# Gates and half of the state turned by transposing transfers, and every transposing read issued from ScalarE's queue

## The chip, the cores and the metric

The kernel runs on one core of a Trainium2 chip. The metric is the time of one execution on the device in microseconds (us); less is better. A time is given as the median of several executions, with the lowest and the highest.

## The reference

One decoder layer on x of 256 tokens x 2048 columns, in float32, with a second input mem of 256 tokens. Cut to what matters:

```python
def swiglu(x, w_gu, w_down):
    g, u = jnp.split(x @ w_gu, 2, axis=-1)
    return (jax.nn.silu(g) * u) @ w_down

h = x
h = h + 0.5 * swiglu(rmsnorm(h, ffn1_norm), ffn1_w_gu, ffn1_w_down)          # 2048 -> 2 x 5632 -> 2048
proj = rmsnorm(h, mix_norm) @ w_in
gu, gv, z, xbc, dt_raw = jnp.split(proj, split_at, axis=-1)
a_out = chunked_sgu(jax.nn.gelu(gu), jax.nn.gelu(gv), gm_v_norm, gm_w_s, gm_b_s)   # u * (W_s norm(v) + b)
m_out = mamba2_group(z, xbc, dt_raw, ...)                                    # conv, chunked scan, gate, norm
h = h + jnp.concatenate([a_out, m_out], axis=-1) @ w_out
h = h + memory_cross_attention(rmsnorm(h, xa_norm), rmsnorm(mem, mem_norm), xa_w_q, xa_w_kv, xa_w_o)
h = h + 0.5 * swiglu(rmsnorm(h, ffn2_norm), ffn2_w_gu, ffn2_w_down)
out = rmsnorm(h, final_norm)
```

"The gates" below are the four 512-column chunks of a_out before the output projection: gelu(u) times the mixed v. "The state" is h, in four chunks h[0] to h[3] of 512 columns, each with its two tiles of 128 tokens.

## The kernel before

**Weights.** All weights are streamed once, in pieces of 256 rows x 1024 columns. `load` issues a piece on SyncE's queue (SP) into one of three buffers `raw`. A float32 product is computed from parts: ScalarE (ACT) casts the piece to a rounded high part `hi` (L169), VectorE (DVE) subtracts it to get the low part `lo` (L177), and TensorE (PE) multiplies the high and low parts into PSUM banks `acc` (L74). There are three buffers for `hi` and two for `lo`. `last_cast` and `last_split` keep the casts on ACT and the low parts on DVE in the order of the code. A plain piece takes PE 24 products of 512 columns. Some pieces ("S") are multiplied in seven products of sums instead (Strassen's scheme): DVE first makes the four sums `sum` (in three operations at L177), both the raw part (1536 columns) and the sums (2048) are then cast and split, and PE needs 21 products.

**Order.** PE's instructions run in the order of the code. Work around the matmuls is put off with `later(fn, by)`: it is emitted by `step()` once `by` further steps are over; there is one step per weight piece (two halves in a plain one).

**Turning.** The left operand of a product needs its contraction axis on the partitions, so each activation is turned in 128x128 blocks. There are two ways:

- On PE: `to_operand` and `Pieces.put` run transposes against an identity matrix into a PSUM bank `tpose` (L77), four for half a chunk of 512 columns x 256 tokens. ACT and DVE then write the high and low parts of the operand (L391 and L393 where a column scale `col` is applied, L385 and L386 or L476 and L477 where not). This way turns the state after the first feed-forward block (`Normed.chunk`, through `operand_later`), the gates (`ats.later`, L959), and other activations.
- By transfers: in the feed-forward blocks the chunk `silu(g)*u` (tiles `part`) is turned by `Pieces.turn_later` (L481). ACT copies each tile into two 16-bit halves (L485, `halves`), POOL's queue writes them to DRAM (`planes`, L487), and one step later SP issues a transposing read of half the chunk (L491) into a tile `turned`, with a second read a half step after it. Four steps after its read the half is put into the operand (`hid`, `hids`) by ACT and DVE. That is done for 22 chunks, 44 reads.

**Places.** In each feed-forward block, `ffn` computes 11 chunks of 512 hidden columns in two runs (5 and 6), each followed by a down projection `add_sum` that adds to h[0] and h[1] in its first half and to h[2] and h[3] in its second. In the second down projection of the first block, `done` (that is `nx.chunk`) hands each chunk of h over as soon as it is final: chunks 0 and 1 are turned while the second half runs, chunks 2 and 3 after it. `Normed.stats` has ACT square h for the norm (L353). The gates are made in two runs of `proj_tok` over the u columns of w_in, two chunks each, and are put off by one and two steps. Scratch tiles of 2 KB per partition (`part`, `gate`, `halves`, `turned`, `junk`, `forms`) share six buffers, `tag="t2k"`.

Of the kernel before, what the change touches and what calls it, by code (L numbers as in the profile page):

```python
# [8 lines left out]
F32 = mybir.dt.float32  # L9
F32R = mybir.dt.float32r  # L10
U16 = mybir.dt.uint16
AF = mybir.ActivationFunctionType
# [35 lines left out]
def hybrid_layer(ctx: ExitStack, tc: tile.TileContext, x, xt, mem, memt, w_gu1, w_dn1, w_in, w_s, w_out,  # L48
# [30 lines left out]
    def later(fn, by=1, bankless=False):  # L79
        put_off.append((steps[0] + by, len(put_off), fn, bankless))  # L80
# [9 lines left out]
    def slot(shape, dtype, name):  # L90
        return big.tile(shape, dtype, name=name, tag="slot")

    def half_k(dtype, name):
        return tmp.tile([P, NC], dtype, name=name, tag="t2k")
# [62 lines left out]
    def behind(instructions):  # L157

        order = ExitStack()
        for ins in instructions:  # L160
            order.enter_context(tc.issue_after(ins))
        return order
# [199 lines left out]
        return r  # L362


    def in_turn(src, last, op):

        if not src.tensor.name.startswith("turned"):
            return op()
        with behind(last):
            ins = op()  # L370
        last[:] = [ins.ins]
        return ins

    def to_operand(srcs, dst, q, c0=None, of=None):
        of = q if of is None else of
        if isinstance(srcs, list):
            ps = side("tpose").rearrange("p (k s) -> p k s", k=2)
            for k in range(2):
                for t in range(NT):
                    transpose(out=ps[:, k, t * P:(t + 1) * P],  # L380
                              in_=srcs[t][:, (of + k) * P:(of + k + 1) * P], identity=ident)
        else:
            ps = srcs
        if c0 is None:
            hi = in_turn(ps, last_cast, lambda: nc.scalar.copy(out=dst[:, q:q + 2, :S], in_=ps))  # L385
            lo = in_turn(ps, last_split, lambda: nc.vector.tensor_tensor(  # L386
                out=dst[:, q:q + 2, S:], in0=ps, in1=dst[:, q:q + 2, :S].bitcast(F32), op=ALU.subtract))
        else:
            scs = [col[:, c0 + of + k:c0 + of + k + 1] for k in range(2)]
            for k in range(2):  # L390
                hi = nc.scalar.activation(dst[:, q + k, :S], ps[:, k, :], AF.Copy, scale=scs[k])  # L391
            for k in range(2):
                lo = nc.vector.scalar_tensor_tensor(out=dst[:, q + k, S:], in0=ps[:, k, :], scalar=scs[k],  # L393
                                                    in1=dst[:, q + k, :S].bitcast(F32),
                                                    op0=ALU.mult, op1=ALU.subtract)
        return hi.ins, lo.ins


    def operand_later(srcs, to, name, c0=None, by=1):
# [13 lines left out]

        later(first, by)

    owed = []


    class Pieces(dict):
        def __init__(self, kinds, name, donor=None):  # L420

            self.kinds, self.name, self.half, self.made, self.donor = kinds, name, None, {}, donor

        def add(self, srcs, q, c0):

# [31 lines left out]
        def sums(self, dst, ps, c0=None):  # L457
            in_sbuf = ps.tensor.name.startswith("turned")
            if not in_sbuf or c0 is not None:
                a = half_k(F32, "forms").rearrange("p (f s) -> p f s", f=4)  # L460
            if in_sbuf and c0 is None:
                a = ps
            elif c0 is None:
                nc.scalar.copy(out=a, in_=ps)
            else:
                for k in range(2):
                    nc.scalar.activation(a[:, 2 * k:2 * k + 2], ps[:, 2 * k:2 * k + 2], AF.Copy,
                                         scale=col[:, c0 + k:c0 + k + 1])

            b = half_k(F32, "forms").rearrange("p (f s) -> p f s", f=4)  # L470
            in_turn(a, last_split, lambda: nc.vector.tensor_tensor(
                out=b[:, 0:2], in0=a[:, 1:2].broadcast_to([P, 2, P]), in1=a[:, 0:4:3], op=ALU.subtract))
            nc.vector.tensor_tensor(out=b[:, 2], in0=a[:, 0], in1=b[:, 1], op=ALU.subtract)
            nc.vector.tensor_tensor(out=b[:, 3], in0=a[:, 2], in1=b[:, 2], op=ALU.subtract)
            for x, f0, f1 in ((a, 0, 4), (b, 4, 8)):
                hi = in_turn(x, last_cast, lambda: nc.scalar.copy(out=dst[:, 0, f0:f1], in_=x))  # L476
                lo = nc.vector.tensor_tensor(out=dst[:, 1, f0:f1], in0=x, in1=dst[:, 0, f0:f1].bitcast(F32),  # L477
                                             op=ALU.subtract)
            return hi.ins, lo.ins

        def turn_later(self, srcs, by):  # L481
            planes = dram.tile([S, 2, NC], U16, name="planes", tag="planes", bufs=2)
            for t in range(NT):
                halves = tmp.tile([P, 2 * NC], U16, name="halves", tag="t2k")
                nc.scalar.copy(out=halves.rearrange("p (b n) -> p b n", b=2),  # L485
                               in_=srcs[t].bitcast(U16).rearrange("p (n b) -> p b n", b=2))
                nc.gpsimd.dma_start(out=planes[t * P:(t + 1) * P].rearrange("p b n -> p (b n)"), in_=halves)  # L487
            for q in (0, 2):
                def fetch(q=q):
                    to = half_k(F32, "turned").rearrange("p (k s) -> p k s", k=KP)  # L490
                    nc.sync.dma_start(out=to.bitcast(U16).rearrange("p k s -> p (k s)").rearrange("p (k s) -> p k s", k=KP),  # L491
                                      in_=planes[:, :, q * P:(q + 2) * P].rearrange("s b n -> (s b) n"), transpose=True)
                    later(lambda: self.put(len(self), to, 0, None), by=by[1], bankless=True)
                later(fetch, by=by[0] + q / 4, bankless=True)

        def later(self, srcs, c0=None, by=1):
            for q in (0, 2):
# [2 lines left out]
    class Normed:  # L500
# [7 lines left out]

        def chunk(self, n, by=1):
            srcs = [h[n][:, t, :] for t in range(NT)]  # L510
            if isinstance(self.xts, Pieces):

                for i in (2 * n, 2 * n + 1):
                    later(lambda i=i: self.xts.put(i, srcs, i % 2 * KP, self.c0 + n * KG),
                          self.bys.get(i, by))
                later(lambda: self.stats(n), self.stats_by)
            else:
                operand_later(srcs, self.xts, f"xt_{self.name}{n}", self.c0 + n * KG, by)
                self.stats(n)
# [59 lines left out]
    def ffn(nrm, w_gu, w_dn, done=None, each=None, fine=0, by_token=False):  # L579
        for c_from, c_to in ((0, 5), (5, 11)):  # L580
            kinds, turn = DN_KINDS[c_to - c_from]
            hts = Pieces(kinds, "hid", nrm.xts)
            for c in range(c_from, c_to):
# [18 lines left out]
                    proj_sum(w_gu, 0, nrm.xts, FIRST_KINDS, (c * NC, DFF + c * NC), mid, evac, FIRST, fine)  # L602
                else:
                    proj_sum(w_gu, 0, nrm.xts, GU_KINDS, (c * NC, DFF + c * NC), mid, evac, GU_ORDER)
                hts.turn_later(gs, (1, 4))
            last = c_to == 11
            add_sum(w_dn, c_from * NC, hts, (kinds, kinds), turn, 0.5, done if last else None, each if last else None,
                    last and by_token)
# [336 lines left out]
    for c in (0, 2):  # L945
# [10 lines left out]

        proj_tok(w_in, 0, nx.xts, (U0 + c * NC, U0 + (c + 1) * NC), evac)
        for j in range(2):
            ats.later(gss[j], by=1 + j)  # L959

    ss_m = small.tile([P, NT, 4], F32, name="ss_m", bufs=1)
    for c in (0, 2):
# [230 lines left out]
```

## Time and profile before

| | |
|---|---|
| median of 3 runs | 2431.74 us (2431.56 to 2431.85) |
| the profiled execution: its time | 2432.23 us |
| its span, first to last instruction | 2430.5 us |
| mean granted clock of PE | 0.999 of full speed |
| busy: PE / DVE / ACT / POOL | 2419.1 / 2033.1 / 1351.7 / 59.0 us |
| moved by DMA | 503.87 MB, mean 207 GB/s |

PE is busy nearly throughout. A busy share says nothing about whether the work was needed, and nothing about a matmul that waits inside its recorded duration, so the rows to read are those of the waits and of the distance from one matmul's start to the next. "PEld" is PE's loading of the stationary operand, which runs beside the matmuls. In rows of the timeline, the first number is the start in us from the span's start and the second the busy time in us; "x4" after a row means four such instructions in a row, and a bracket says how long the engine was idle before the row and on what it waited. In rows of a queue ("SPq"), the busy time is the time in which the engine's queue issued the transfer. In groups of instructions, three numbers like 270/272/273 are the least, the median and the longest duration in ns.

### The profile page before, as it was taken

The page shows a single profiled execution, that of the slowest core. Times are in us where ns is not written, and L with a number is a line of the kernel's source. Part 1 is how long each engine was busy: PE and PEld are TensorE (multiplying, and loading weights), DVE is VectorE, ACT ScalarE, POOL GpSimd, SP SyncE. Part 2 cuts the span into 40 slices and gives each one's busy share as a digit, 9 for nine tenths or more (in the row PEclk, how much of TensorE's full clock was granted, in tenths as well). Part 3 has the DMA queues.
Part 4 walks back from the last instruction along what each step waited for, and adds up shares of the span by engine and source line. Part 5 has one row for each costly group of instructions (what it writes and reads, how often), then busy time and mean ns, then how long its engine had stood idle before and what let it go on. Part 6 is the DMA issues. An engine that isn't in the chain of part 4 may idle for free.

```text
span 2430.5 us, 29042 instructions
## 1 busy us (share of the span) xinstructions
PE 2419.1 (100%) x11189; PEld 2014.9 (83%) x11189; DVE 2033.1 (84%) x1943; ACT 1351.7 (56%) x1251; POOL 59.0 (2%) x112
## 2 busy tenths in 40 slices
PE   9999999999999999999999999999999999999998
PEld 7888888888888888788888888888888888888887
DVE  8999889999877777655698888778899988899997
ACT  7565446565556555435555655555556554556554
POOL 1000000000000000000000000000000000000000
PEclk9999999999999999999999999999999999999999
DMA  8767667677555555545566655555567666776774
GB/s 302 238 221 232 205 208 232 221 232 227 196 186 189 189 185 179 204 160 187 182 203 231 232 187 165 174 182 181 187 213 240 225 213 203 223 226 226 232 220 154
DMA packets 251211, 503.87 MB, mean 207 GB/s; under 512 B 62896, under 2 KB 64976, under 8 KB 250304
## 3 DMA queue, kind: packets, MB, share of 16 engines
q1 hardware_dynamic: 243552, 475.86, 60.6%
q0 software_dynamic: 6688, 25.12, 2.8%
q8 instruction: 87, 1.43, 0.2%
q10 hardware_dynamic: 832, 1.05, 0.1%
q14 instruction: 52, 0.43, 0.1%
HBM read 476.76 MB, written 13.66 MB: 202 GB/s over the span
## 4 chain that ended last, share of the span: by engine, by line
PE 94%; issue 3%; DVE 1%; ACT 1%; DMA 0%; POOL 0%; SPq 0%; POOLq 0%; DVEq 0%; ACTq 0%
PE acc L74 91%; PE tpose L77 1%; PE yp L74 1%; PE o L74 0%; PE logits L74 0%; DVE lo L177 0%; ACT hi L169 0%; DVE sum L177 0%; PE mixed L74 0%; DMA raw<-in_w_gu 0%; PE dt L74 0%; DVE part L568 0%; PE scores L74 0%; PE yo L74 0%; PE st L74 0%
## 5 line engine op out<-in xcount | busy, mean ns | idle before, releaser
L177 DVE TENSOR_TENSOR lo<-raw,hi 128x2048 fp32r<-128x2048 f32 (+2 forms) x449 | 944.8, 2106 | 251.6 <-PE acc L74 194.7
L169 ACT CAST hi<-raw 128x2048 fp32r<-128x2048 f32 (+1 forms) x437 | 785.2, 1798 | 504.9 <-PE acc L74 447.1
L74 PE MATMUL acc<-hi,xp_ffn 128*128 128x512 f32 x1824 | 573.8, 389 | 0.0
L74 PEld LDWEIGHTS acc<-hi,xp_ffn 128*128 128x128 f32 x1824 | 342.3, 188 | 71.6 <-ACT hi L191 0.6
L169 ACT CAST hi<-sum 128x2048 fp32r<-128x2048 f32 x117 | 224.1, 1916 | 296.1 <-DVE sum L177 158.2
L74 PE MATMUL acc<-lo,xp_ffn 128*128 128x512 f32 x912 | 355.0, 389 | 1.4 <-DVE h L629 1.2
L177 DVE TENSOR_TENSOR lo<-sum,hi 128x2048 fp32r<-128x2048 f32 x117 | 268.1, 2291 | 36.7 <-ACT hi L169 36.7
L74 PE MATMUL acc<-hi,hid 128*128 128x512 f32 x896 | 281.9, 389 | 0.0
L74 PE MATMUL acc<-hi,xt_mix 128*128 128x512 f32 x768 | 242.6, 393 | 0.0
L74 PEld LDWEIGHTS acc<-lo,xp_ffn 128*128 128x128 f32 x912 | 171.2, 188 | 37.6 <-DVE h L629 1.6
L568 DVE TENSOR_TENSOR part<-acc,part 128x512 f32<-128x512 f32 x272 | 180.4, 685 | 24.1 <-PE acc L74 8.7
L74 PEld LDWEIGHTS acc<-hi,hid 128*128 128x128 f32 x896 | 168.2, 188 | 34.9
L74 PE MATMUL acc<-lo,hid 128*128 128x512 f32 x448 | 174.3, 389 | 0.0
L74 PEld LDWEIGHTS acc<-hi,xt_mix 128*128 128x128 f32 x768 | 144.2, 188 | 30.6 <-issue 1.0
L177 DVE TENSOR_TENSOR sum<-sum,raw 128x512 f32<-128x512 f32 x234 | 161.4, 690 | 6.2
L74 PE MATMUL acc<-lo,xt_mix 128*128 128x512 f32 x384 | 149.6, 390 | 0.0
L74 PE MATMUL acc<-hi,xp_ffn1s 128*128 128x512 f32 x466 | 148.5, 389 | 0.0
L74 PE MATMUL acc<-hi,xp_ffn2s 128*128 128x512 f32 x466 | 148.5, 389 | 0.0
L177 DVE TENSOR_TENSOR sum<-raw 128x1024 f32<-128x1024 f32 x117 | 142.4, 1217 | 0.4 <-DMA raw<-in_w_gu 0.4
L74 PE MATMUL acc<-xt_mix,hi 128*128 128x512 f32 x512 | 140.5, 396 | 0.0
L74 PE MATMUL acc<-hi,hids 128*128 128x512 f32 x392 | 125.2, 389 | 0.0
L74 PE MATMUL acc<-hi,memt 128*128 128x512 f32 x384 | 123.4, 392 | 0.0
(294 smaller groups left out, 3157.8 us busy)
## 6 DMA issues: line engine op xcount, KB each, us to landing
raw<-in_w_gu SPq DMA_DIRECT2D x284, 512.0 KB, 4.4
raw<-in_w_in SPq DMA_DIRECT2D x80, 1024.0 KB, 5.1
raw<-in_w_dn SPq DMA_DIRECT2D x60, 1024.0 KB, 5.1
raw<-in_w_gu SPq DMA_DIRECT2D x136, 256.0 KB, 4.7
raw<-in_w_kv SPq DMA_DIRECT2D x24, 1024.0 KB, 5.3
raw<-in_w_out SPq DMA_DIRECT2D x21, 1024.0 KB, 5.1
raw<-in_w_dn SPq DMA_DIRECT2D x28, 512.0 KB, 4.1
raw<-in_w_dn SPq DMA_DIRECT2D x56, 256.0 KB, 4.5
```

The costliest lines, as they stand in the source:

```text
L74: return pe(nc.tensor.matmul(out, lhsT=lhsT, rhs=rhs, start=start, stop=stop))
L77: return pe(nc.tensor.transpose(out=out, in_=in_, identity=identity))
L169: last_cast[:] = [nc.scalar.copy(out=t[:, :n], in_=x[:, :n]).ins]
L177: last_split[:] = [nc.vector.tensor_tensor(**kw).ins]
L568: nc.vector.tensor_tensor(out=out, in0=a, in1=b, op=op)
```

## The change

- `write_planes`, `read_turned` and `turn_over` take the place of `turn_later`'s body: the copies and the writes are as before, but the reads are issued by ACT (`nc.scalar.dma_start`) and not by SP, each ordered behind the latest cast of ACT (`last_cast`). `planes` gets four buffers in place of two.
- The gates are turned by transfers (`ats.turn_later`): the two chunks of a run are read 4 and 5.5 steps after they are made, their second halves half a step later, and put 2.5 steps after that.
- Chunks 0 and 1 of h, after the first feed-forward block, are turned by transfers (`operand_turned`), with the same delays. Chunks 2 and 3 stay on PE.
- The chunks of the feed-forward blocks are read 3.5 steps after they are made, no longer 1, and put 2.5 steps after that, no longer 4.
- `in_turn` now also orders operations with a column scale, from C_MIX on, behind the latest cast or low part.

So 32 transposes of gates and 16 of the 96 of h leave PE; the writes of planes from POOL's queue go from 44 to 56, and the transposing reads from 44 on SP's queue to 56 on ACT's.

```diff
@@ -362,9 +362,34 @@
 
-    def in_turn(src, last, op):
-
-        if not src.tensor.name.startswith("turned"):
+    def write_planes(srcs, n=NC):
+        planes = dram.tile([len(srcs) * P, 2, n], U16, name="planes", tag="planes", bufs=4)
+        for t, src in enumerate(srcs):
+            halves = tmp.tile([P, 2 * n], U16, name="halves", tag="t2k")
+            nc.scalar.copy(out=halves.rearrange("p (b n) -> p b n", b=2),
+                           in_=src.bitcast(U16).rearrange("p (n b) -> p b n", b=2))
+            nc.gpsimd.dma_start(out=planes[t * P:(t + 1) * P].rearrange("p b n -> p (b n)"), in_=halves)
+        return planes
+
+    def read_turned(to, planes, c0, n):
+        with behind(last_cast):
+            last_cast[:] = [nc.scalar.dma_start(
+                out=to, in_=planes[:, :, c0:c0 + n].rearrange("s b n -> (s b) n"), transpose=True).ins]
+
+    def turn_over(srcs, by, put):
+        planes = write_planes(srcs)
+
+        def fetch(q):
+            to = half_k(F32, "turned")
+            read_turned(to.bitcast(U16).rearrange("p (k s) -> p k s", k=KP), planes, q * P, KP * P)
+            later(lambda: put(to.rearrange("p (k s) -> p k s", k=KP), q), by=by[1], bankless=True)
+
+        for q in (0, 2):
+            later(lambda q=q: fetch(q), by=by[0] + q / 4, bankless=True)
+
+    def in_turn(src, last, op, c0=None):
+
+        if not src.tensor.name.startswith("turned") or c0 is not None and c0 < C_MIX:
             return op()
@@ -388,11 +413,12 @@
             for k in range(2):
-                hi = nc.scalar.activation(dst[:, q + k, :S], ps[:, k, :], AF.Copy, scale=scs[k])
+                hi = in_turn(ps, last_cast, lambda k=k: nc.scalar.activation(
+                    dst[:, q + k, :S], ps[:, k, :], AF.Copy, scale=scs[k]), c0)
             for k in range(2):
-                lo = nc.vector.scalar_tensor_tensor(out=dst[:, q + k, S:], in0=ps[:, k, :], scalar=scs[k],
-                                                    in1=dst[:, q + k, :S].bitcast(F32),
-                                                    op0=ALU.mult, op1=ALU.subtract)
+                lo = in_turn(ps, last_split, lambda k=k: nc.vector.scalar_tensor_tensor(
+                    out=dst[:, q + k, S:], in0=ps[:, k, :], scalar=scs[k], in1=dst[:, q + k, :S].bitcast(F32),
+                    op0=ALU.mult, op1=ALU.subtract), c0)
         return hi.ins, lo.ins
@@ -413,6 +439,19 @@
 
+    def operand_turned(srcs, to, name, c0=None, by=(1, 4)):
+        at = len(to) + sum(1 for o in owed if o is to)
+        owed.append(to)
+
+        def put(src, q):
+            if q == 0:
+                owed.remove(to)
+                assert len(to) == at
+                to.append(slot([P, KG, 2 * S], F32R, name))
+            to_operand(src, to[at], q, c0)
+
+        turn_over(srcs, by, put)
+
     owed = []
@@ -420,6 +459,7 @@
             self.kinds, self.name, self.half, self.made, self.donor = kinds, name, None, {}, donor
+            self.due = 0
@@ -464,12 +504,12 @@
                 for k in range(2):
-                    nc.scalar.activation(a[:, 2 * k:2 * k + 2], ps[:, 2 * k:2 * k + 2], AF.Copy,
-                                         scale=col[:, c0 + k:c0 + k + 1])
+                    in_turn(ps, last_cast, lambda k=k: nc.scalar.activation(
+                        a[:, 2 * k:2 * k + 2], ps[:, 2 * k:2 * k + 2], AF.Copy, scale=col[:, c0 + k:c0 + k + 1]), c0)
 
             b = half_k(F32, "forms").rearrange("p (f s) -> p f s", f=4)
-            in_turn(a, last_split, lambda: nc.vector.tensor_tensor(
-                out=b[:, 0:2], in0=a[:, 1:2].broadcast_to([P, 2, P]), in1=a[:, 0:4:3], op=ALU.subtract))
+            in_turn(ps, last_split, lambda: nc.vector.tensor_tensor(
+                out=b[:, 0:2], in0=a[:, 1:2].broadcast_to([P, 2, P]), in1=a[:, 0:4:3], op=ALU.subtract), c0)
             nc.vector.tensor_tensor(out=b[:, 2], in0=a[:, 0], in1=b[:, 1], op=ALU.subtract)
@@ -478,20 +518,11 @@
 
-        def turn_later(self, srcs, by):
-            planes = dram.tile([S, 2, NC], U16, name="planes", tag="planes", bufs=2)
-            for t in range(NT):
-                halves = tmp.tile([P, 2 * NC], U16, name="halves", tag="t2k")
-                nc.scalar.copy(out=halves.rearrange("p (b n) -> p b n", b=2),
-                               in_=srcs[t].bitcast(U16).rearrange("p (n b) -> p b n", b=2))
-                nc.gpsimd.dma_start(out=planes[t * P:(t + 1) * P].rearrange("p b n -> p (b n)"), in_=halves)
-            for q in (0, 2):
-                def fetch(q=q):
-                    to = half_k(F32, "turned").rearrange("p (k s) -> p k s", k=KP)
-                    nc.sync.dma_start(out=to.bitcast(U16).rearrange("p k s -> p (k s)").rearrange("p (k s) -> p k s", k=KP),
-                                      in_=planes[:, :, q * P:(q + 2) * P].rearrange("s b n -> (s b) n"), transpose=True)
-                    later(lambda: self.put(len(self), to, 0, None), by=by[1], bankless=True)
-                later(fetch, by=by[0] + q / 4, bankless=True)
+        def turn_later(self, srcs, by, c0=None, at=None):
+            if at is None:
+                at = self.due
+                self.due += 2
+            turn_over(srcs, by, lambda to, q: self.put(at + q // 2, to, q, c0))
@@ -508,7 +539,10 @@
             srcs = [h[n][:, t, :] for t in range(NT)]
-            if isinstance(self.xts, Pieces):
+            if n < 2 and not isinstance(self.xts, Pieces):
+                operand_turned(srcs, self.xts, f"xt_{self.name}{n}", self.c0 + n * KG, (4 + 1.5 * n, 2.5))
+                self.stats(n)
+            elif isinstance(self.xts, Pieces):
@@ -602,7 +636,7 @@
                     proj_sum(w_gu, 0, nrm.xts, GU_KINDS, (c * NC, DFF + c * NC), mid, evac, GU_ORDER)
-                hts.turn_later(gs, (1, 4))
+                hts.turn_later(gs, (3.5, 2.5))
             last = c_to == 11
@@ -956,7 +990,7 @@
         for j in range(2):
-            ats.later(gss[j], by=1 + j)
+            ats.turn_later(gss[j], (4 + 1.5 * j, 2.5))
```

**PE, in the second half of the second down projection** (a piece of the difference; `hi,hid` and `lo,hid` are the down projection's products, h_90 and h_91 the chunks 0 and 1 of h):

```order
-L74 MATMUL acc<-hi,hid 128x512
-L77 MATMUL tpose<-ident,h_90 128x128 x4
-L77 MATMUL tpose<-ident,h_91 128x128 x4
-L74 MATMUL acc<-hi,hid 128x512
-L74 MATMUL acc<-lo,hid 128x512
-L74 MATMUL acc<-hi,hid 128x512 x2
-L74 MATMUL acc<-lo,hid 128x512
-L74 MATMUL acc<-hi,hid 128x512 x2
-L74 MATMUL acc<-lo,hid 128x512
-L74 MATMUL acc<-hi,hid 128x512 x2
-L74 MATMUL acc<-lo,hid 128x512
-L74 MATMUL acc<-hi,hid 128x512
```

Of each of the two groups of eight transposes nothing is left in this place; the matmuls on both sides follow each other directly. The four groups of the gates go in the same way from between the products of the second u run and of the z run.

**ACT, one chunk of a feed-forward block,** from the copies of a chunk to the first put of its turned data. Before:

```order
L485 COPY halves<-part 128x1024 x2
L169 CAST hi<-sum 128x2048
L169 CAST hi<-raw 128x2048
L169 CAST hi<-raw 128x1536
L169 CAST hi<-sum 128x2048
L476 CAST hids<-turned 128x512
```

And after:

```order
L369 COPY halves<-part 128x1024 x2
L169 CAST hi<-sum 128x2048
L169 CAST hi<-raw 128x2048
L376 DMA_TRANSPOSE turned<-planes 128x2x512 x2
L169 CAST hi<-raw 128x1536
L169 CAST hi<-sum 128x2048
L169 CAST hi<-raw 128x2048
L516 CAST hids<-turned 128x512
```

The pair of reads now stands between two casts of weights, and the first put has moved behind one more cast.

**ACT at the turn to the mixer,** from the first half's end of the second down projection on (ss_mix are the sums of squares of h; xt_mix is the turned state). Before:

```order
L169 CAST hi<-raw 128x2048 x2
L353 ACTIVATE junk,ss_mix<-h_90 128x512 x2
L353 ACTIVATE junk,ss_mix<-h_91 128x512
L169 CAST hi<-raw 128x1536
L353 ACTIVATE junk,ss_mix<-h_91 128x512
L169 CAST hi<-sum 128x2048
L391 ACTIVATE xt_mix_4811<-tpose,col 128x256 x2
L391 ACTIVATE xt_mix_4821<-tpose,col 128x256 x2
L169 CAST hi<-raw 128x2048
```

And after:

```order
L369 COPY halves<-h_90 128x1024 x2
L353 ACTIVATE junk,ss_mix<-h_90 128x512 x2
L369 COPY halves<-h_91 128x1024
L169 CAST hi<-raw 128x1536
L369 COPY halves<-h_91 128x1024
L353 ACTIVATE junk,ss_mix<-h_91 128x512 x2
L169 CAST hi<-sum 128x2048
L169 CAST hi<-raw 128x2048
L376 DMA_TRANSPOSE turned<-planes 128x2x512
L169 CAST hi<-raw 128x1536
L169 CAST hi<-sum 128x2048
L376 DMA_TRANSPOSE turned<-planes 128x2x512
```

Four copies have joined the squares, the reads stand between the casts that follow, and the operations that write xt_mix (L391 before, L416 after) have moved behind them.

## The prediction

> **What bounds the kernel now.** I read the page first, its share of busy time and its chain of work:
>
> ```profile
> PE 2419.1 (100%) x11189; PEld 2014.9 (83%) x11189; DVE 2033.1 (84%) x1943; ACT 1351.7 (56%) x1251; POOL 59.0 (2%) x112
> ...
> PE 94%; issue 3%; DVE 1%; ACT 1%; DMA 0%; POOL 0%; SPq 0%; POOLq 0%; DVEq 0%; ACTq 0%
> ```
>
> PE is busy for all but 11 us, and 94% of the chain that ended last is PE's own work. A busy matmul may still be a late one, so the next view is the waits of PE alone:
>
> ```profile
> PE acc L74 <- DVE h L629: 1.2, 1, 1.2
> PE acc L74 <- DVE lo L177: 0.2, 1, 0.2
> ```
>
> There is almost nothing in it after the start. The stages by windows, with busy us of PE, PEld, DVE, ACT, POOL and the granted clock:
>
> ```profile
> 400.00:640.00 240.00, 240.00 (x1064) 198.84 (x1063) 222.13 (x200) 139.54 (x110) 5.42 (x10) 1.00 0.71 225
> 1057.00:1110.00 53.00, 53.00 (x249) 44.16 (x248) 29.45 (x24) 24.05 (x22) 0.00 (x0) 1.00 0.58 194
> ```
>
> In the feed-forward stage DVE is busy 222 of 240 us, so it has little room; in the gate stage it is busy 29 of 53. The clock is granted in full in both. So time is won by whatever leaves PE's stream, as long as DVE and ACT still hand over each weight piece in time.
>
> **What leaves PE.** Transposes of the gates (32) and of half of the state (16 of the 96 of h) go, 48 in all. The timeline and the chain show what they cost:
>
> ```profile
> L77 PE MATMUL tpose<-ident,gate x32: 270/272/273, 1057.9 to 1110.3; 128*128 128x128 f32 x32
> ...
> 1057.93 1.03 PE L77 MATMUL tpose<-ident,gate 128*128 128x128 f32 x8
> ...
> 1060.40 0.39 PE L74 MATMUL acc<-lo,xt_mix 128*128 128x512 f32 x1
> ...
> 1061.76 0.39 PE L74 MATMUL acc<-lo,xt_mix 128*128 128x512 f32 x1
> ...
> 1064.26 1.03 PE L77 MATMUL tpose<-ident,gate 128*128 128x128 f32 x8
> ```
>
> ```profile
> 639.09 0.87 PE tpose L77 x8
> 639.97 2.75 PE acc L74 x12
> 642.72 0.87 PE tpose L77 x8
> ...
> 1109.73 0.87 PE tpose L77 x8
> ```
>
> The 272 ns of one transpose is latency; they overlap. What counts is the distance of starts. Six matmuls run between 1060.40 and 1061.76, so one takes 0.2267 us. From the start of one gate group of 8 to the next (6.33 us) there are 24 matmuls, 5.44 us, so a group costs 0.89 us. For the state, 639.09 to 642.72 (3.63 us) holds 12 matmuls, 2.72 us, so a group costs 0.91 us. There are four gate groups and two state groups: 4 x 0.89 + 2 x 0.91 = **5.38 us**, all of it on the path, since PE stands in every link of the chain there. The Trainium skill, "VectorE: DVE Perf Modes", section "The three transpose paths", gives 390 ns for a 128x128 bf16 transpose on TensorE and 1309 ns by the DMA crossbar, and its rules for authors prefer TensorE where PSUM will do; by these figures 48 transposes would lose 44 us, as an estimate. That needs the DMA to be on the path and a transpose to cost its full latency; the rows above show 0.11 us for each on a saturated engine.
>
> **What is added.** For every 512-wide chunk turned by transfers: two copies into 16-bit halves on ACT, two writes from POOL's queue, two transposing reads. Six chunks gain this (four of gates, two of state): 12 copies, 12 writes, 12 reads. And all 56 reads, the 44 old ones too, now stand in ACT's order behind the latest weight cast, where SP issued them before.
>
> ```profile
> L485 ACT COPY halves<-part x44: 1036/1046/1051, 57.0 to 2301.5; 128x1024 uint16<-128x1024 uint16 x44
> ...
> L491 SPq DMA_TRANSPOSE turned<-planes x44: 1231/1294/3448, 62.1 to 2308.6; - x44
> ...
> L109 SPq DMA_DIRECT2D turned<-in_xt x6: 368/374/453, 5.7 to 18.5; - x6
> ...
> L109 ACTq DMA_DIRECT2D turned<-in_xt x2: 475/482/488, 0.8 to 1.3; - x2
> ...
> planes<-halves POOLq DMA_DIRECT2D x44, 256.0 KB, 4.5
> ```
>
> The copies are 12 x 1.05 = 12.6 us of ACT, which is idle 44% of the span. No row shows a transposing read issued by ACT. Its price lies between nothing beyond SP's 1.29 us and SP's longest, 3.45 us; a plain load costs ACT 0.482 us and SP 0.374, a factor of 1.29, so I take 1.29 x 1.294 = 1.67 us (an estimate). It cannot be a gain on ACT, which issued none. 56 x 1.67 is 94 us of ACT's time, which throughput bears easily: 1352 + 13 + 94 is 60% of the span. What matters is what stands behind it in ACT's order: the next cast of weights, then DVE's low part, then PE. One cycle of the feed-forward stage:
>
> ```profile
> 99.03 1.92 ACT L169 CAST hi<-sum 128x2048 fp32r<-128x2048 f32 x1 [0.28 <-DVE sum L177]
> 100.86 1.91 ACT L169 CAST hi<-raw 128x2048 fp32r<-128x2048 f32 x1
> 104.01 1.49 ACT L169 CAST hi<-raw 128x1536 fp32r<-128x1536 f32 x1 [1.25 <-PE acc L74]
> 108.79 1.91 ACT L169 CAST hi<-sum 128x2048 fp32r<-128x2048 f32 x1 [3.29 <-PE acc L74]
> ```
>
> ```profile
> 108.60 1.75 DVE L177 TENSOR_TENSOR lo<-raw,hi 128x1536 fp32r<-128x1536 f32 x1
> 110.73 2.29 DVE L177 TENSOR_TENSOR lo<-sum,hi 128x2048 fp32r<-128x2048 f32 x1 [0.39 <-ACT hi L169]
> ```
>
> ```profile
> 102.01 2.59 SPq L491 DMA_TRANSPOSE turned<-planes  x2
> ```
>
> In the new order the pair of reads stands between the cast of 100.86 and that of 104.01. ACT gets there at 102.77; the plane had landed by 102.01, when SP began. Two issues of 1.67 end at 106.1, the cast of 1.49 us at 107.6, and DVE wants it at 108.60. So the pair fits into idle time that ACT spends waiting for PE, with 1 us to spare. SP, free of the pair, issues weights earlier; PE never waited for those, so I put that at nothing. The turned data are put one step later than before (due 6 steps after the gates, not 5), still before the piece that needs them.
>
> **The start.** Near 83 us the chain runs through DVE and ACT, and PE is late once:
>
> ```profile
> 75.77 0.68 DVE L386 TENSOR_TENSOR hid<-turned,hid 128x512 fp32r<-128x512 f32 x1
> ...
> 81.10 2.29 DVE L177 TENSOR_TENSOR lo<-sum,hi 128x2048 fp32r<-128x2048 f32 x1 [0.39 <-ACT hi L169]
> ```
>
> ```profile
> 82.69 0.61 PE L74 MATMUL acc<-hi,xp_ffn1s 128*128 128x512 f32 x2
> 83.45 0.50 PE L74 MATMUL acc<-lo,xp_ffn1s 128*128 128x512 f32 x1
> ```
>
> Two matmuls take 0.45 us, the third starts 0.76 us on, so 0.31 is lost, 0.46 by the time PE is back in pace. The new order puts the DVE operation of 75.77 behind the low part of 81.10, which brings that 0.6 us forward. So 0 to 0.46 us is won; I take half, 0.23.
>
> **The turn to the mixer** is the tightest new place. Four copies of h (4.2 us) join ACT's squares of h after the first half of the second down projection, and four reads follow between casts.
>
> ```profile
> 631.00 0.63 ACT L353 ACTIVATE junk<-h 128x512 f32<-128x512 f32 x1 [0.83 <-DVE h L528]
> ...
> 639.03 1.91 ACT L169 CAST hi<-sum 128x2048 fp32r<-128x2048 f32 x1 [1.80 <-DVE sum L177]
> ```
>
> ```profile
> 643.18 3.45 DVE L393 SCALAR_TENSOR_TENSOR xt_mix<-tpose,col,xt_mix 128x256 fp32r<-128x256 f32 x8
> ...
> 666.62 1.76 DVE L177 TENSOR_TENSOR lo<-raw,hi 128x1536 fp32r<-128x1536 f32 x1 [3.13 <-PE acc L74]
> ...
> 672.05 2.29 DVE L177 TENSOR_TENSOR lo<-raw,hi 128x2048 fp32r<-128x2048 f32 x1 [1.47 <-issue]
> ...
> 678.99 2.29 DVE L177 TENSOR_TENSOR lo<-sum,hi 128x2048 fp32r<-128x2048 f32 x1 [0.39 <-ACT hi L169]
> ```
>
> ```profile
> 683.13 0.39 PE L74 MATMUL acc<-lo,hids 128*128 128x512 f32 x1
> ```
>
> Started at 631.00, when the first h is there, the copies and squares put the cast of 639.03 at about 640.3, which DVE's earlier freedom absorbs. DVE's 3.45 us for xt_mix leaves 643 and lands, piece by piece, around 662 to 674, where DVE waits 3.13 + 1.47 us. The low part of 678.99 ended at 681.28 and PE wanted it at 683.13. Without two groups PE is 1.81 us earlier there, wanting it at 681.3. Laying the new order out with these durations and 1.6 us a read, I get DVE's end at 680.6: slack shrinks from 1.85 to about 0.7 us, an estimate, but holds. The last two chunks keep their transposes, and the gate stage has spare DVE time (29 of 53 us).
>
> **Sum.** The profiled execution took 2432.23 us (span 2430.5 plus 1.73 around it), 0.49 above the median of 2431.74. 2432.23 - 5.38 - 0.23 = 2426.62; on the median's footing 2426.13. I give **2426.1 us**, 0.23% less.
>
> **Rivals.** *A stall at a transition*: the 0.7 us at 681 is overdrawn, or a copy of a gate waits for the buffer of an earlier one whose write has not landed (4.5 us). For it speaks the thin slack, against it that later pieces recover. Price 0.8 to 5 us, so 2427 to 2431; I put its centre at 2429. *ACT's queue becomes the bound, slower than before*: in the cycle above the pair may take 108.60 - 102.77 - 1.49 = 4.34 us before DVE is late. How long PE then holds out is shown by
>
> ```profile
> 116.23 0.39 PE L74 MATMUL acc<-lo,xp_ffn1s 128*128 128x512 f32 x1
> ```
>
> the sum part ready at 113.02 is first used at 116.23, so 3.2 us more. A read thus decides from (4.34 + 3.2) / 2 = 3.8 us on, and loses more than the whole gain from about 3.9. At 4.5 us each cycle loses 9.0 - 7.5 = 1.5 us, 22 cycles 32 us: 2458. Against it stands SP's longest of 3.45 and its usual 1.29. *The transposes were hidden anyway*: then 2431.7; the chain with PE in every link speaks against it, and I count it with the first rival.
>
> **How the numbers follow.** Forecast 0.62 (2425.2 to 2426.9); stall at a transition, or a hidden gain, 0.27; ACT the bound 0.11. A measurement of this kernel can tell about 0.2%, 4.9 us, from no change, so faster means below 2426.9: chances 0.62, 0.27 and 0.11 are those of the three cases. The range 2425.2 to 2431 takes in the forecast, with the whole start gain, and most of the stalls; it leaves out the last case and the worst of the second.
>
> **What would show it.** Right: no transposes of the gates and 80 of h, PE busy about 2413.5 us, no PE wait above 0.5 us after 90 us, reads on ACT's queue near 1.7 us, and the distance from 82.69 to the third matmul back to 0.45. Wrong: waits of PE on the low parts of L177 near 681, 1060 or 1105, or once per feed-forward chunk; a wait of ACT's reads for the writes of planes above 1 us in each cycle; reads of 3.8 us or more.

## The result, and the profile after

| | before | after |
|---|---|---|
| median | 2431.77 us (2431.46 to 2432.56, 6 runs) | 2442.92 us (2440.45 to 2449.29, 6 runs) |
| the profiled execution | 2432.23 us, span 2430.5 | 2442.03 us, span 2440.3 |

The ratio is 1.0052, 95% interval 1.0042 to 1.0062: slower by 0.52%, where 0.23% faster was forecast, and outside the range given. The scatter grew too, from 1.1 to 8.8 us.

The changed kernel's page, the busy time of the engines and the chain by engine:

```profile
PE 2418.7 (99%) x11141; PEld 2013.3 (83%) x11141; DVE 2033.8 (83%) x1943; ACT 1360.4 (56%) x1261; POOL 67.0 (3%) x124
PE 95%; issue 3%; ACT 1%; DVE 1%; DMA 0%; POOL 0%; SPq 0%; POOLq 0%; DVEq 0%; ACTq 0%
```

The 48 transposes are gone (11189 to 11141 instructions), yet PE's busy time fell by 0.4 us and not by 5.4. The busy share does not say why. The waits of PE lead to it:

```profile
PE acc L74 <- DVE lo L177: 10.4, 3, 4.1
PE idle L74 <- DVE idle L668: 1.3, 1, 1.3
PE acc L74 <- DVE h L663: 1.0, 1, 1.0
```

Where PE had waited 0.2 us for a low part, it now waits 10.4 us in three places. The first of them in PE's timeline:

```profile
522.71 0.39 PE L74 MATMUL acc<-hi,xp_ffn 128*128 128x512 f32 x1
526.43 0.50 PE L74 MATMUL acc<-lo,xp_ffn 128*128 128x512 f32 x1 [3.34 <-DVE lo L177]
...
528.10 0.63 PE L74 MATMUL acc<-lo,xp_ffn 128*128 128x512 f32 x1
528.53 1.05 PE L74 MATMUL acc<-hi,xp_ffn 128*128 128x512 f32 x2
529.38 0.63 PE L74 MATMUL acc<-lo,xp_ffn 128*128 128x512 f32 x1
```

The wait is only part of the loss: behind it, matmuls start 0.43 us apart (528.10 to 528.53; two from 528.53 to 529.38) and not 0.227. That is why the busy time did not fall: slow matmuls count as busy. The windows behind the three stalls, and one after recovery, give PE's granted clock (the third value from the end; the first is the length of the window):

```profile
526.40:531.40 5.00, 4.97 (x15) 3.92 (x16) 4.11 (x6) 1.32 (x2) 0.00 (x0) 0.66 0.78 261
531.40:540.00 8.60, 8.60 (x40) 7.09 (x39) 7.94 (x10) 4.30 (x5) 1.08 (x2) 1.00 0.59 199
1151.60:1156.10 4.50, 4.47 (x13) 3.56 (x14) 2.98 (x3) 0.62 (x1) 0.00 (x0) 0.62 0.74 244
2257.70:2261.90 4.20, 4.14 (x11) 3.26 (x12) 3.22 (x5) 1.32 (x2) 0.00 (x0) 0.59 0.72 219
```

Each of these three stalls is followed by 4 to 5 us at about 0.6 of the clock, so some 1.7 us more are lost (5.00 x (1 - 0.66), 4.50 x (1 - 0.62), 4.20 x (1 - 0.59)). What DVE did before the first, in its timeline:

```profile
515.32 2.29 DVE L177 TENSOR_TENSOR lo<-sum,hi 128x2048 fp32r<-128x2048 f32 x1 [0.39 <-ACT hi L169]
517.53 0.68 DVE L517 TENSOR_TENSOR hids<-turned,hids 128x512 fp32r<-128x512 f32 x1
520.61 0.69 DVE L602 TENSOR_TENSOR part<-acc,part 128x512 f32<-128x512 f32 x1 [2.40 <-ACT part L568]
521.76 2.09 DVE L602 TENSOR_TENSOR part<-acc,part 128x512 f32<-128x512 f32 x3 [0.46 <-DVE part L602]
523.76 0.41 DVE L511 TENSOR_TENSOR forms<-turned 128x256 f32<-128x256 f32 x1
524.09 2.29 DVE L177 TENSOR_TENSOR lo<-raw,hi 128x2048 fp32r<-128x2048 f32 x1
```

ACT, over the same stretch:

```profile
518.19 1.91 ACT L169 CAST hi<-raw 128x2048 fp32r<-128x2048 f32 x1 [0.57 <-ACT hi L169]
520.01 0.57 ACT L568 COPY part<-acc 128x512 f32<-128x512 f32 x1
```

The low part at 524.09 could have started when its cast ended, at 520.1, and DVE stood idle from 518.2 to 520.6. It could not go ahead: `in_turn` holds the first subtraction of a turned half's sums (L511) behind the previous low part and holds the next low part behind L511, and on DVE L511 stands behind four operations (L602) that add up PE's products, the first of them by way of ACT's copy (L568), which came behind a cast. So PE waits for a low part which waits for PE's own earlier products. In the order of before, the same half was put one step earlier. Its subtraction (L471 there) stood ahead of the weight sums of that piece, and the next operation on PE's products (L568 there) came only 10 us later:

```profile
511.48 0.42 DVE L471 TENSOR_TENSOR forms<-turned 128x256 f32<-128x256 f32 x1
511.81 1.22 DVE L177 TENSOR_TENSOR sum<-raw 128x1024 f32<-128x1024 f32 x1
...
521.93 1.47 DVE L568 TENSOR_TENSOR part<-acc,part 128x512 f32<-128x512 f32 x2 [0.35 <-ACT part L534]
```

The place follows from the step. A second half is now put at the end of the last S piece of the next chunk; there the four L602 of that piece have been emitted already. It matters only where that half is of kind S. In the second run (kinds CCCCSCCSCCSS) the odd places 7 and 11 are S, and only 7, the fourth chunk, meets another chunk's L602. That is one stall in each feed-forward block, at 522 and 2254 us. The third, before 1151.62, is the same with the gates: here the last S half stands behind the multiplications by the z gates (L1002), which wait for ACT's work on PE's products (L1000).

```profile
1147.54 0.69 DVE L1002 TENSOR_TENSOR y<-y,gate 128x512 f32<-128x512 f32 x1 [1.37 <-ACT gate L1000]
1148.15 0.42 DVE L511 TENSOR_TENSOR forms<-turned 128x256 f32<-128x256 f32 x1
```

### The profile page after: what moved, and what is told of

It reads as the page before. It is cut to its first block, busy times and chain, and to the rows that moved or that the text cites. A ratio compares the mean times of both kernels' runs of the same rounds, so it can differ in the third digit from the quotient of the medians.

```text
span 2440.3 us, 28964 instructions
## 1 busy us (share of the span) xinstructions
PE 2418.7 (99%) x11141; PEld 2013.3 (83%) x11141; DVE 2033.8 (83%) x1943; ACT 1360.4 (56%) x1261; POOL 67.0 (3%) x124
## 4 chain that ended last, share of the span: by engine, by line
PE 95%; issue 3%; ACT 1%; DVE 1%; DMA 0%; POOL 0%; SPq 0%; POOLq 0%; DVEq 0%; ACTq 0%
PE acc L74 91%; PE tpose L77 1%; PE yp L74 1%; PE logits L74 0%; PE o L74 0%; DVE lo L177 0%; ACT hi L169 0%; PE mixed L74 0%; DMA raw<-in_w_gu 0%; PE dt L74 0%; PE scores L74 0%; PE yo L74 0%; PE st L74 0%; ACT hi L191 0%; DVE part L602 0%
## 5 line engine op out<-in xcount | busy, mean ns | idle before, releaser
L602 DVE TENSOR_TENSOR part<-acc,part 128x512 f32<-128x512 f32 x272 | 180.8, 686 | 30.5 <-ACT part L568 11.9
```

The source lines that it names most:

```text
L602: nc.vector.tensor_tensor(out=out, in0=a, in1=b, op=op)
```

## The experiments

Theory A says that the three stalls come from that order on DVE. Theory B says that they come from ACT's queue, where a read holds up the casts.

### The puts earlier: in the feed-forward blocks, for the gates, and both

The first edit takes half a step from the put of the feed-forward chunks:

```diff
-                hts.turn_later(gs, (3.5, 2.5))
+                hts.turn_later(gs, (3.5, 2))
```

> The feed-forward chunks are put into the operand 2 steps after their read in place of 2.5, so that the second half comes one piece earlier, ahead of the products of the last S piece. Theory A (order on DVE): the two stalls near 522 and 2254 us of the changed kernel come from one subtraction on DVE that stands behind four operations waiting for PE, with the next low part behind it; they go, the one at 1147 stays. The two cost about 5.1 + 4.7 us with the slow matmuls behind them, so about 2443 - 9.7 = 2433 us. Theory B (ACT's queue: reads issued by ACT make the casts late): nothing is moved off ACT, so the stalls stay, 2440 to 2445 us.

The second reads the gates one step earlier and takes half a step from their put:

```diff
-            ats.turn_later(gss[j], (4 + 1.5 * j, 2.5))
+            ats.turn_later(gss[j], (3 + 1.5 * j, 2))
```

> The gates are read after 3 and 4.5 steps and put 2 later, so that the last pieces come ahead of the end of the first z run. Theory A: the stall at 1147 us goes, the two in the feed-forward blocks stay; it cost about 5.8 us, so about 2437 us. Theory B: the stalls stay, 2440 to 2445 us.

The third kernel has both edits.

> Both edits. Theory A: no PE wait above 1 us after the start, 2426 to 2428 us, what the sum of the prediction gives without the stalls. Theory B: 2440 to 2445 us. If the median lies between (2430 to 2436), some third cost is in the change that the three stalls don't hold.

Measured: 2435.3 us (2432.63 to 2443.98, 10 runs), 2440.83 (2439.68 to 2441.79, 5 runs) and 2431.22 (2429.18 to 2434.43, 11 runs; ratio 0.9998, interval 0.9990 to 1.0007). The first lost the stalls at 522 and 2254 and kept the third, as A has it; its median is 2.3 us above A's 2433, and its executions spread over 11 us. The second missed A's 2437: the stall at 1147 went, but a new one of 2.72 us came at 1119. Both edits together landed between the theories; the new stall, here of 2.52 us, is the third cost that the expectation left room for. The kernel with both edits in ACT's timeline (rows "ACTq" are reads being issued) and in DVE's:

```profile
1103.80 4.44 ACTq L376 DMA_TRANSPOSE turned<-planes  x1
1108.35 1.91 ACT L169 CAST hi<-raw 128x2048 fp32r<-128x2048 f32 x1 [2.65 <-issue]
1111.23 3.14 ACTq L376 DMA_TRANSPOSE turned<-planes  x2
1114.41 0.62 ACT L516 CAST ats<-turned 128x512 fp32r<-128x512 f32 x1 [4.16 <-issue]
1114.94 1.90 ACT L169 CAST hi<-raw 128x2048 fp32r<-128x2048 f32 x1
```

```profile
1115.07 0.69 DVE L517 TENSOR_TENSOR ats<-turned,ats 128x512 fp32r<-128x512 f32 x1 [7.05 <-ACT ats L516]
1115.67 2.28 DVE L177 TENSOR_TENSOR lo<-raw,hi 128x2048 fp32r<-128x2048 f32 x1
```

One read took 4.44 us to issue and the next two 3.14 together, and the casts behind them came late. PE waited for the low part of 1115.67. Its cast, that of 1108.35, had ended at 1110.3; what it stood behind on DVE is L517, the low part of a turned half, and L517 waited for the cast of that half (L516), which the two reads held up. So ACT's queue, theory B, makes this stall, and the order on DVE hands it on to PE.

### All reads on SP

```diff
-        with behind(last_cast):
-            last_cast[:] = [nc.scalar.dma_start(
-                out=to, in_=planes[:, :, c0:c0 + n].rearrange("s b n -> (s b) n"), transpose=True).ins]
+        nc.sync.dma_start(out=to, in_=planes[:, :, c0:c0 + n].rearrange("s b n -> (s b) n"), transpose=True)
```

> The changed kernel with all 56 reads issued by SP in place of ACT, at the same steps. Theory A: the order on DVE is the same, so the three stalls stay, 2440 to 2445 us. Theory B: the stalls go with ACT's reads, about 2427 us.

Measured: 2443.69 us (2443.07 to 2444.74, 5 runs). The three stalls stand where they were, at 523, 1147 and 2255, with 10.5 us of waits in place of 10.4. So the queue did not make them; A holds. The scatter fell from 8.8 us (6 executions) to 1.7 (5), which points to the queue as its cause.

> Puts of the feed-forward chunks and of the gates earlier, and all 56 reads on SP. With both edits and the reads on ACT, 2431.2 us were left, scattered over 5 us, with one stall at 1115 us behind reads that took up to 4.4 us to issue on ACT. Theory A with B for the rest (reads on ACT block the casts where they crowd): no PE wait above 1 us, 2425.5 to 2427.5 us, and a scatter of about 1 us like that of the kernel before. If ACT's queue costs nothing, 2429 to 2432 as with the reads on ACT.

This is the same edit with both puts earlier: 2427.77 us (2427.07 to 2429.30, 11 runs; ratio 0.9984, interval 0.9975 to 0.9993). The only waits of PE left are in the first 25 us. The median is just above the range expected.

### The ordering edge taken out

```diff
-            in_turn(ps, last_split, lambda: nc.vector.tensor_tensor(
-                out=b[:, 0:2], in0=a[:, 1:2].broadcast_to([P, 2, P]), in1=a[:, 0:4:3], op=ALU.subtract), c0)
+            nc.vector.tensor_tensor(
+                out=b[:, 0:2], in0=a[:, 1:2].broadcast_to([P, 2, P]), in1=a[:, 0:4:3], op=ALU.subtract)
```

> The changed kernel with one ordering edge taken out: the first subtraction of the sums of a turned half is no longer held between two low parts of weights on DVE. It still comes late, but the low parts may pass it. Theory A: the stall is made by the edge, so all three stalls go, 2426 to 2431 us (the upper end for what ACT's reads cost in some executions). If the late put itself were the cause (data not there), the stalls would stay: 2440 to 2445 us.

Measured: 2427.38 us (2425.97 to 2438.22, 11 runs; ratio 0.9985, interval 0.9976 to 0.9994). At the change's own steps, with one edge less, the three stalls are gone. The median is in A's range; two of the eleven executions lie above it. The profiled one was the slowest, 2438.22, and shows what the upper end is made of: two stalls of PE in the gate stage, of 1.71 us at 1095 and of 8.04 before 1130.99. The group of the gates' reads on ACT (least, median, longest ns), and rows of ACT's and DVE's timelines:

```profile
L376 ACTq DMA_TRANSPOSE turned<-planes x8: 1242/3366/7926, 1059.1 to 1121.6; - x8
```

```profile
1113.68 13.67 ACTq L376 DMA_TRANSPOSE turned<-planes  x2
1127.39 0.62 ACT L516 CAST ats<-forms 128x512 fp32r<-128x512 f32 x1 [11.90 <-issue]
```

```profile
1128.04 0.69 DVE L517 TENSOR_TENSOR ats<-forms,ats 128x512 fp32r<-128x512 f32 x1 [5.31 <-ACT ats L516]
1128.65 2.29 DVE L177 TENSOR_TENSOR lo<-raw,hi 128x2048 fp32r<-128x2048 f32 x1
```

Two reads held ACT for 13.67 us. Behind them came the cast of a turned half, behind that its low part on DVE, and behind that the low part for which PE waited; the cast of that one had ended at 1115.5. The same eight reads took 1508 ns at the median in the profiled execution of the changed kernel. How long such an issue takes differs between executions; what it waits for, the trace does not show.

### The queue alone, at the old and at the new step

Gates and state go back to PE (`n < 0`, `ats.later`), the 44 old reads stay on ACT:

```diff
-            if n < 2 and not isinstance(self.xts, Pieces):
+            if n < 0 and not isinstance(self.xts, Pieces):
-                hts.turn_later(gs, (3.5, 2.5))
+                hts.turn_later(gs, (1, 4))
-            ats.turn_later(gss[j], (4 + 1.5 * j, 2.5))
+            ats.later(gss[j], by=1 + j)
```

> Of the change the queue alone: the 44 old reads issued by ACT behind the latest cast, at the old steps (1 and 4); gates and state turned on PE as before. If reads on ACT cost nothing in the feed-forward stage, as the prediction had it: 2431 to 2432.5 us. If their issue delays casts there in some cycles: 2433 to 2440 us, with a wider scatter.

Measured: 2606.89 us (2606.05 to 2607.70, 4 runs), 175 us more than before and far outside both expectations. ACT's timeline, in one chunk:

```profile
103.35 1.05 ACT L369 COPY halves<-part 128x1024 uint16<-128x1024 uint16 x1 [0.51 <-DVE part L631]
107.06 1.24 ACTq L376 DMA_TRANSPOSE turned<-planes  x1
108.48 1.90 ACT L169 CAST hi<-raw 128x2048 fp32r<-128x2048 f32 x1 [4.08 <-issue]
```

The issue itself is short, 1.24 us, but from the end of the copy at 104.4 to 107.06 ACT waits for the write of the planes (issued at 104.69, with a median of 2.3 us from issue to landing), with the casts queued behind. In the kernel before, with these reads on SP, PE has no such wait. PE stalls in all 22 chunks and runs slowly after each; its waits:

```profile
PE acc L74 <- ACT hi L169: 74.7, 22, 5.5
PE acc L74 <- DVE lo L177: 37.3, 22, 1.8
```

The same kernel with `(3.5, 2)` in place of `(1, 4)`:

> Of the change the queue and the later read alone: 44 reads issued by ACT, 3.5 steps after the chunk, put 2 steps later; gates and state turned on PE. With the read 1 step after the chunk ACT waited for the write of the planes with the next cast behind it, and 175 us were lost. If that wait is the whole cost, it is gone here: 2431 to 2432.5 us. If issuing on ACT costs by itself, 2433 or more.

Measured: 2431.43 us (2431.17 to 2435.51, 10 runs; ratio 1.0001, interval 0.9992 to 1.0010). The wait is gone and so is its cost. So the move to ACT needs the later read, and the later read, put 2.5 steps on, is what made the stalls.

### Only the gates' reads on SP

Both puts earlier, and in `turn_over` and `read_turned`:

```diff
+        on_sp = srcs[0].tensor.name.startswith("gate")
...
+        if on_sp:
+            nc.sync.dma_start(out=to, in_=planes[:, :, c0:c0 + n].rearrange("s b n -> (s b) n"), transpose=True)
+            return
```

> Both puts earlier, the 8 reads of the gates on SP, the 48 others on ACT. If the reads on ACT cost time only where they crowd (the gate stage, where eight reads and eight copies stand between a few casts), no stall is left: 2425.5 to 2428 us with a scatter of 1 us. If reads on ACT delay casts in the feed-forward stage too, the scatter of 5 us and 2429 to 2432 stay.

Measured: 2427.14 us (2426.34 to 2431.38, 11 runs; ratio 0.9983, interval 0.9975 to 0.9992), the profiled execution 2426.46. PE has no wait behind the first 25 us. The median is as expected; the scatter of 1 us is not, since one of the eleven is still at 2431.38 and another at 2429.38. The same with the puts left late, and the edge taken out instead:

> The changed kernel with its own steps for reads and puts, the ordering edge of the sums' first subtraction taken out, and the 8 reads of the gates on SP. With the edge out and all reads on ACT the profiled execution took 2438 us, 8.2 us of it one PE stall behind reads of the gates that ACT took up to 7.9 us to issue, while most executions took 2426 to 2428. If the edge and the gates' reads on ACT are all that is wrong with the change, no stall is left at its own steps: 2425.5 to 2428 us, no execution above 2431. If the late puts cost by themselves, 2429 or more.

Measured: 2427.0 us (2426.13 to 2431.09, 10 runs; ratio 0.9983, interval 0.9973 to 0.9992), no wait of PE behind the start. So the late puts cost nothing by themselves. One execution at 2431.09 just missed what was expected; both kernels show one such in some ten, neither of them profiled, and its cause is open.

Both kernels use two queues for transposing reads. The Trainium skill, "DMA: Bandwidth & Descriptors", section "Silent corruption: two transposing streams in flight at once", says that such reads of two queues must not be in flight together. Here they are apart by hundreds of us (SP's from 1059 to 1112 us, ACT's up to about 655 and again from 1780), and no run here tried it otherwise.

### More turned by transfers

As the kernel with both puts earlier and all reads on SP, and:

```diff
-        mts.later(gs, C_SSM + c * KG)
+        mts.turn_later(gs, (3, 2), C_SSM + c * KG)
```

> As the kernel with both puts earlier and the reads on SP, and the four chunks of the other group (y, 32 transposes after the z runs) are turned by transfers too. If a group of eight transposes costs PE 0.9 us wherever it stands, 4 x 0.9 = 3.6 us less than that kernel, about 2423 us; a new stall at the turn to the output projection, where the first of these pieces is needed 8 steps on, would give it back: 2426 or more.

Measured: 2435.92 us (2434.08 to 2437.48, 11 runs), 8 us more than the kernel that it was built on. Four groups of transposes are gone, and PE waits at the turn to the output projection:

```profile
PE acc L74 <- DVE lo L177: 7.3, 7, 2.5
```

There DVE and ACT scale these halves and make their sums between the weight pieces. The seven stalls, with what follows them, gave back the 3.6 us and 8 more.

### Stalls of six lengths

The question here is whether the slow stretch grows with the stall, or begins at some length of idleness. Fills of a small tile on DVE are put into the kernel before, ahead of one plain piece's split in six chunks of the second feed-forward block:

```diff
+                if i == 4 and w is w_gu2:
+                    for _ in range(FILL.get(cs[0] // NC, 0)):
+                        with behind(last_split):
+                            last_split[:] = [nc.vector.memset(idle, 0.0).ins]
...
+    FILL = {2: 16, 3: 20, 4: 24, 6: 28, 7: 34, 8: 40}
```

> The kernel before, with 16, 20, 24, 28, 34 and 40 fills of a small unused tile put on DVE ahead of the low part of one plain piece in six chunks of the second feed-forward block. At about 0.21 us a fill and 2.6 us of slack at that piece (0.5 at the last S piece behind it), PE should stall by about 0.8, 1.6, 2.4, 3.3, 4.5 and 5.8 us there, and about 2 us more at the S piece. In the changed kernel matmuls started 0.43 us apart and not 0.227 for some 4 us after stalls of 3.1 to 4.3 us, and not after one of 1.2. If the slow pace comes only from a certain length of idleness on, the short stalls show none and the longer ones the same 1.5 us of loss; if it grows with the stall, 0.3 to 2.5 us.

Measured: 2490.02 us, one execution. A fill took 0.39 us and not 0.21, so the stalls are longer than expected, 2.71 to 12.11 us, and the short ones that the question needed are missing. (The changed kernel's own stalls, by its timeline, were of 2.98 to 4.12 us.) The first and the fifth of them in PE's timeline, and the windows behind them:

```profile
1836.63 0.50 PE L74 MATMUL acc<-lo,xp_ffn 128*128 128x512 f32 x1 [2.71 <-DVE lo L177]
...
2186.91 0.80 PE L74 MATMUL acc<-lo,xp_ffn 128*128 128x512 f32 x1 [9.76 <-DVE lo L177]
```

```profile
1836.60:1841.10 4.50, 4.47 (x13) 3.49 (x14) 4.16 (x4) 1.83 (x2) 0.00 (x0) 0.64 0.70 230
2186.90:2193.00 6.10, 6.09 (x15) 4.84 (x16) 5.66 (x5) 3.45 (x3) 0.00 (x0) 0.52 0.64 189
```

The shorter stalls are in other kernels. With both puts earlier:

```profile
1118.01 0.50 PE L74 MATMUL acc<-lo,xt_mix 128*128 128x512 f32 x1 [2.52 <-DVE lo L177]
```

```profile
1118.00:1123.00 5.00, 4.99 (x22) 4.10 (x23) 4.24 (x6) 3.48 (x4) 0.00 (x0) 1.00 0.65 210
```

With more turned by transfers:

```profile
1232.38 0.50 PE L74 MATMUL acc<-lo,mts 128*128 128x512 f32 x1 [2.49 <-DVE lo L177]
```

```profile
1232.30:1237.30 5.00, 4.92 (x15) 3.90 (x16) 5.00 (x9) 4.97 (x9) 0.00 (x0) 0.66 0.65 211
```

And with the gates alone put earlier, where the feed-forward stall stayed:

```profile
526.82 0.50 PE L74 MATMUL acc<-lo,xp_ffn 128*128 128x512 f32 x1 [3.35 <-DVE lo L177]
```

```profile
526.80:531.80 5.00, 4.98 (x22) 4.13 (x23) 5.00 (x8) 1.33 (x2) 0.00 (x0) 1.00 0.78 271
```

After 2.71 us of idleness the clock was 0.64 for 4.5 us, after 9.76 it was 0.52 for 6.1. So the slow stretch does not grow in step with the stall: behind the six stalls of the ladder it cost 1.6 to 2.9 us (4.50 x 0.36, 6.10 x 0.48). But no single length of idleness marks its beginning. After 2.49 us it came (0.66), after 2.52 it did not (1.00); and after 3.35 us at 526 it did not come, where the changed kernel, after 3.34 us at the same place, ran at 0.66. What decides it besides the length is not shown.

## Why the prediction was wrong, step by step

- **What bounds the kernel: right.** PE sets the time throughout; the gains and losses that were profiled are what PE gained, waited, or ran slowly.
- **The groups of transposes, 5.38 us: right; the start, 0.23: right in kind.** The same instruction, the last matmul, stands in the timelines of before, of after, and of the kernel without stalls (gates' reads on SP) at:

```profile
2421.56 0.39 PE L74 MATMUL acc<-hi,hid 128*128 128x512 f32 x1
```

```profile
2431.09 0.39 PE L74 MATMUL acc<-hi,hid 128*128 128x512 f32 x1
```

```profile
2415.51 0.39 PE L74 MATMUL acc<-hi,hid 128*128 128x512 f32 x1
```

  The stall-free kernel is 6.05 us ahead of before, against 5.61 forecast. Of these, 0.65 are won by 85 us, and 5.40 behind that, where the transposes went. PE is busy for 2413.6 us, against the 2413.5 forecast, and the profiled execution took 2426.46 us, against 2426.62. So the transposes were not hidden. The late matmul near 83 us follows after 0.46 us in the changed kernel, as forecast, and after 0.62 in the stall-free one. The changed kernel stands 15.58 us behind that one; its three stalls come to 10.4 us, and the slow matmuls after them to 5.1. (At 85 us it was still 0.65 us ahead of it, so about as much is lost in places that were not found.) 15.58 - 6.05 = 9.53 us, and the profiled executions of the changed kernel and of before differ by 9.80.
- **Reads on ACT: right where the prediction looked, not elsewhere.** The read took 1344 ns at the median, less than the 1.67 us taken; the longest, 4042, in the second feed-forward block, is above the bound of 3.45 taken from SP:

```profile
L376 ACTq DMA_TRANSPOSE turned<-planes x56: 1241/1344/4042, 61.1 to 2316.9; - x56
```

  In the feed-forward stage the pair fits between two casts, as the cycle at 99 us was read, and costs nothing that can be measured (2431.43, with single reads of up to 4.65 us). In the gate stage no cycle was laid out, since DVE had spare time there; ACT's casts behind the reads were the thin place, and added stalls in profiled executions of three kernels with the gates' reads on ACT. That the 8.8 us of scatter of the changed kernel come from there is likely, but its slowest executions were not profiled.
- **The turn to the mixer: right.** No stall at 681 in any kernel with chunks 0 and 1 turned by transfers.
- **"The turned data are put one step later than before ..., still before the piece that needs them": this step failed.** It was costed at nothing by asking when the data are needed. What counted was where the put lands in DVE's order: behind four operations that wait for PE, and, through the edge of `in_turn`, ahead of the next weights' low part. With the slow matmuls, the two feed-forward stalls are 9.7 us of the 15.58 and the gates' 5.8. Taking the edge out, or putting the halves earlier, removes them; moving the reads to SP does not.
- **The rivals.** "A stall at a transition" had the right kind of event and both wrong causes (the slack at 681, a copy that waits for a buffer), and a price for one stall of up to 5 us, without the slow clock behind it. "ACT's queue becomes the bound" was priced by the length of an issue; the 175 us at the old step show that the wait in front of an issue can cost far more. "The transposes were hidden anyway" is refuted by the 6.05 us.

One cycle was read and taken for all 22. It was one whose second half is of kind C; the chunk that stalls is one of eleven in each block.

## What to carry to other kernels

When work is put off by a step, follow it in the order of each engine it runs on, in every distinct cycle and not in a typical one: an operation chained between two pieces of critical work makes them wait for whatever stands before it. Here an instruction that issues a transfer from ACT's queue blocked ACT for its wait and for its issue; move one there only where its data have landed and where the work behind it can wait for the longest issue seen. And price a stall of a saturated TensorE with the slow clock that may follow it, not by its length alone.

## What was not expected of the hardware

- **A stall of PE can cost more than its length.** Behind most stalls of 2.49 to 12.11 us, the clock falls for some us; in the windows shown, 4.2 to 6.1 us at 0.52 to 0.66 of it; behind one of 2.52 and one of 3.35 us the clock stayed full, as it did behind those of up to 1.82 us in the kernel with more turned by transfers. The Trainium skill, "TensorE: Matmul & The Clock Gate", section "What's actually happening", puts the drop to half rate after one idle window of about 3.4 us; here it came after 2.49 and 2.71 us too.
- **Issuing a transposing read took ACT from 1.24 to 7.93 us** for the same shape. The longest were in the gate stage; where only the feed-forward chunks were read by ACT, they reached 4.65. On SP they took up to 4.65 us as well. What lengthens them is not shown.
